# A two-layer hybrid transformer step on one core: rotations and square sums from GpSimd to VectorE, a norm of other instructions, and a second layer with three heads ahead of its norm

## The chip, the core and the metric

One core of a Trainium2 chip runs the whole step in one launch. The engines named below are TensorE (PE, with its weight loads PEld), VectorE (DVE), ScalarE (ACT), GpSimd (POOL) and SyncE (SP), which issues the DMAs. Times are microseconds on the device; lower is better. The metric is the device time of one execution, median of several runs.

## The reference, cut to what matters

Two layers run over 384 tokens of width 1024: 128 context tokens and 256 latent tokens, which share all weights but have their own modulation vectors (shift, scale, gate). Of one layer, for the latent tokens (for the context tokens the same, without rotation and cache):

```python
sa, ca, ga, sm, cm, gm = jnp.split(mod_s, 6, axis=-1)
h = _rmsnorm(xs, norm_mix[d]) * (1.0 + ca) + sa
q, k, v, gb, gc, xin, u, vs = _project(h, w_in[d])
q = _apply_axial_rope(q, rope)
k = _apply_axial_rope(k, rope)
k_all = jnp.concatenate([cache_k[:, d].astype(k.dtype), k], axis=1)
v_all = jnp.concatenate([cache_v[:, d].astype(v.dtype), v], axis=1)
att = _diff_attention(q, k_all, v_all, lam, subln[d], lam_init)
conv = gb * _short_conv(gc * xin, conv_w[d], conv_b[d])
cmlp = _chunk_mlp(u, vs, w_s[d], b_s[d])
xs = xs + ga * (jnp.concatenate([att, conv, cmlp], axis=-1) @ w_out[d])
h = _rmsnorm(xs, norm_mlp[d]) * (1.0 + cm) + sm
xs = xs + gm * _mlp(h, w_up[d], w_down[d])
```

There are four heads with two 64-wide components each. Attention takes, for each component, a softmax over the keys, and combines the two as p0 - lambda * p1. The MLP is a squared ReLU of width 4096.

## The kernel before, in words

**Layout.** Activations are kept transposed: `x` is 128 partitions x 8 tiles (`kt` or `dt`) x 384 tokens. Products have nearly fp32 accuracy: each operand is split into a high and a low part (`hh`, `hl` for activations, `whi`, `wlo` for weights), and `mm3` (L216 to L222) issues three matmuls, high by high, high by low, low by high. Weights come as chunks of 512 KB (`raw`, six buffers); ACT casts a chunk to `whi` (L201), and two ticks later DVE subtracts to get `wlo` (L203), four buffers each. A chunk's successor is begun where the chunk has been used (`refill`).

**What sets the order.** All engines but SP run their instructions in the order in which the program writes them down. That order comes from a heap of Python generators: `start(gen, delay)` puts one in, `go` runs one up to its next `yield`, and `tick()` advances the clock by one after each three-matmul step of a projection (in `proj_tokens` with a width of 512: four ticks for a tile `kt`, nine matmuls). A `yield n` gives the generator its next turn n ticks later. The table `WAIT` holds all these delays as (first layer, second layer). So a delay decides where an instruction stands in its engine's queue, and in that queue it blocks everything behind it until its inputs are there.

**A layer.** The K and Q projections of the first `NPRE` heads ("pkq") do not wait for the norm: they multiply x * scale as it is, with the shift as two more columns (386 instead of 384), and 1/rms (`rstd`) is applied when the result leaves PSUM (`evict`, L514 to L522; `evict_all` L628). Their heads are then finished by `first_heads` (L695 to L713): bias on ACT (L705, L710, L711), `keys` (L660), `queries` (L679). Meanwhile `normed` (L355 to L378) overwrites `hh` and `hl`, tile by tile, with the normed activations: on DVE two products x * scale * rstd, one for each token group (L361), on ACT two halves that add the shift and round to `hh` (L369), on DVE two subtractions to `hl` (L372). From there all projections read the normed parts: V for all heads ("nat", L433 to L455), the remaining heads (`later_heads`, "pk" and "pq", L715 to L726), the convolution, the chunk mixer, then the output projection (three products "po" or "po2"), the up projection ("pup") and the down projection ("pdn").

**Heads.** `keys` rotates K's latent part (`rope_apply`, L652 to L658: a shuffle on DVE, two products and a sum on GpSimd), casts it on ACT (kh, L673, L676) and subtracts on DVE (kl, L677); `queries` does the same for Q (qs, L689, L692). `attention(h, u)` (L730) treats the 128 tokens of unit u: scores (L737, or L740 and L741), maxima on DVE (nm, L745), exponentials on ACT with their sums (e, L750), the two components combined on ACT and DVE (L756, L758), transposes on PE (pt, L762), copies on ACT (atp, ats, L771, L773), and after unit 2 the product with V (po, L785). Units start every 8 ticks and heads every 24, from `unit0` ticks after the start of V on. Score tiles, transposes and statistics share three PSUM buffers ("misc"); projections share four ("acc").

**Square sums.** `stat_tile` (L327 to L336) squares a tile of x on ACT (sq, L329) and adds it to `sacc`; in the MLP parts the add is done by GpSimd (L336), and a product with ones (pstat, L346), two activations (L349, L350) and three DVE instructions (L340 to L342) turn it into `rstd`.

**Hidden units.** `hidden` (L917 to L930) copies two shift columns (`ub`, on DVE), multiplies by `rstd` (DVE), applies ReLU with that bias and a square on ACT, and splits into `ah` and `al`.

Of the kernel before, what the change touches and what calls it, by code (L numbers as in the profile page):

```python
# [15 lines left out]
P = 128  # L16
# [12 lines left out]
NPRE = (3, 2)  # L29
# [33 lines left out]
    "fh0": (14, 14),  # L63
# [8 lines left out]
    "normed": (3, 3),  # L72
    "wait_normed": (1, 12),
    "mix": (4, 4),
    "heads": (4, 1),
# [4 lines left out]
    "unit0": (24, 24),  # L80
    "head": (24, 24),
    "late": (0, 5),
# [18 lines left out]
def dit_kernel(ctx, tc, xT, cT, wmod, wmodT, wall, ck, cv, ws, lam, bs_in, small, rope, ident_in, yT, kT_out, v_out):  # L101
# [112 lines left out]
    def temp(name):  # L214
        return work.tile([P, T], F32, name=name, tag="tA", bufs=4)
# [111 lines left out]
    def stat_tile(dt, eng=nc.gpsimd):  # L327
        sq = temp("sq")
        nc.scalar.activation(sq, x[:, dt, :], AF.Square)  # L329
# [14 lines left out]
    def rstd_of_x():  # L344
        pm = misc_tile("pstat")
        mm(pm[:, 0:T], ones_d, stat["acc"], start=True, stop=True)  # L346
        y = stat["rstd"] = work.tile([P, T], F32, name="rstd", bufs=1)
# [7 lines left out]
    def normed(scale, shift, every):  # L355


        def times(dt):
            t = temp("t")
            for g, a, b in GROUPS:  # L360
                nc.vector.scalar_tensor_tensor(  # L361
                    t[:, a:b], x[:, dt, a:b], scale[:, dt, g : g + 1], stat["rstd"][:, a:b], ALU.mult, ALU.mult
                )
            return t

        t = times(0)
        for dt in range(KT):
            for g, a, b in GROUPS:
                nc.scalar.activation(hh[:, dt, a:b], t[:, a:b], AF.Identity, bias=shift[:, dt, g : g + 1])  # L369
            ahead = times(dt + 1) if dt + 1 < KT else None  # L370
            for g, a, b in GROUPS:
                nc.vector.scalar_tensor_tensor(  # L372
                    hl[:, dt, a:b], t[:, a:b], shift[:, dt, g : g + 1], hh[:, dt, a:b].bitcast(F32),
                    ALU.add, ALU.subtract,
                )
# [132 lines left out]
    for d in range(DEPTH):  # L508
# [26 lines left out]

        if d == 0:
# [42 lines left out]
            for f in range(PARTS - 1):  # L581
# [12 lines left out]
                for dt in (2 * f, 2 * f + 1):  # L594
                    stat_tile(dt, eng=nc.vector)
                if f == 0:
                    next(spread)
            for dt in (KT - 2, KT - 1):
                stat_tile(dt, eng=nc.vector)
# [7 lines left out]
            start(shifted(), 1)  # L607
            start(steps(spread, 4, 3), wt["spread"])
            start(rstd_of_x(), wt["rstd"])
            q_t, k_t, v_t, cv_t, wsT, vsn = mixer_tiles()  # L610
# [12 lines left out]
        else:  # L623
# [4 lines left out]
            def evict_all(i):  # L628
                nc.vector.tensor_copy(bias[:, i], pre[i][:, T:TE])
                evict(i)  # L630

            for i in range(2):
                start(once(evict_all, i), 1 + i)

# [9 lines left out]
        def split_y(i, yf):  # L644
            nc.scalar.copy(y[:, 0, i], yf)
            yield wt["sy"]
            nc.vector.tensor_sub(y[:, 1, i], yf, y[:, 0, i].bitcast(F32))

        LO, HI = slice(0, 64), slice(64, 128)
        parts = {}  # L650

        def rope_apply(t):  # L652
            rt = work.tile([P, 2, TS], F32, name="rt", tag="rope", bufs=1)
            s, t1 = rt[:, 0], rt[:, 1]
            nc.vector.stream_shuffle(s, t, [(i + 16) % 32 for i in range(32)])
            nc.gpsimd.tensor_mul(t1, t, rp[:, 0])
            nc.gpsimd.tensor_mul(s, s, rp[:, 1])
            nc.gpsimd.tensor_add(t, t1, s)  # L658

        def keys(h):  # L660


            k = k_t[:, h % 3]
            nc.sync.dma_start(k[:, TP : 2 * TP], ck[d, h])
            nc.sync.dma_start(kT_out[d, h], k[:, 0:TP])
            yield wt["k0"]
            rope_apply(k[:, 2 * TP :])
            yield wt["k1"]
            kh = work.tile([P, 2, T], F32R, name="kh")
            kl = kl_t[h % 2]  # L670
            parts[h] = [kh, kl]
            for c, own in enumerate((LO, HI)):
                nc.scalar.copy(kh[own, c], k[own, TP:])  # L673
            yield wt["k2"]
            for c, (own, other) in enumerate(((LO, HI), (HI, LO))):
                nc.scalar.copy(kh[other, c], k[own, TP:])  # L676
                nc.vector.tensor_sub(kl[own, c], k[own, TP:], kh[own, c].bitcast(F32))  # L677

        def queries(h):  # L679


            q = q_t[:, h % 3]
            yield wt["q0"]
            rope_apply(q[:, TP:T])
            yield wt["q1"]
            qs = work.tile([P, 2, TS], F32R, name="qs")
            parts[h].append(qs)
            for c, own in enumerate((LO, HI)):
                nc.scalar.copy(qs[own, c], q[own, TP:T])  # L689
            yield wt["q2"]  # L690
            for c, (own, other) in enumerate(((LO, HI), (HI, LO))):
                nc.vector.tensor_sub(qs[other, c], q[own, TP:T], qs[own, c].bitcast(F32))  # L692

        def first_heads():
            for h in range(NPRE[d]):  # L695
                if h != 1:
                    if d == 0:
                        yield from shift_products(raws, bias, 2 * h, 2 * h + 4 - h)
                    qb = bias[:, 2 * h + 1 : 2 * h + 4 - h : 2]
                    nc.vector.tensor_scalar_mul(qb, qb, 0.125)  # L700
                if h == 2:
# [409 lines left out]
```

## Time and profile before

| | |
|---|---|
| time, median of 3 runs | 910.35 (909.78 to 910.5) |
| the profiled execution | 911.23 |
| its span in the profile | 909.4 |
| granted TensorE clock, mean of the span | 0.994 |
| instructions | 14510 |
| share busy: PE, DVE, ACT, POOL | 97%, 72%, 53%, 9% |
| share of the chain that ended last: PE, DVE, ACT, POOL | 84%, 7%, 3%, 2% |
| weights and data read | 153 MB, 171 GB/s over the span |

All places are given in microseconds from the start of the span. The first layer's input side lies at about 56 to 130, the second layer's begins at about 473 and lasts to about 600. A row of a timeline reads: start, duration, engine, line, operation, output<-input, shape, how many alike stand in it, and in square brackets the idle time of the engine ahead of it with what ended that. Where a row holds several instructions ("x2"), its duration is for all of them. A matmul's duration is longer than its place in the pipeline: the distance from one start to the next is what it costs.

### The profile page before, as it was taken

To read this page: it belongs to the slowest core of one execution; us is meant where nothing else is said; L and a number is where in the kernel's file an instruction comes from. 1 tells how busy PE (TensorE), PEld (TensorE's weight loads), DVE (VectorE), ACT (ScalarE), POOL (GpSimd) and SP (SyncE) were. 2 spreads that over 40 slices of the span, in tenths; PEclk is the share of its full clock that TensorE was granted. 3 is DMA by queue.
4 is the path that set the end of the run, shared out by engine and by line. 5 is a ranking of instruction groups with operands and counts; after the bars stand their busy time and mean duration, and the time that the engine had idled before them with its cause. 6 is when DMAs were issued, how large, how long until landed. Compare 5 with 4: busy or idle time off the path is not lost.

```text
span 909.4 us, 14510 instructions
## 1 busy us (share of the span) xinstructions
PE 881.9 (97%) x5476; PEld 841.0 (92%) x5476; DVE 651.5 (72%) x1214; ACT 480.9 (53%) x949; POOL 84.2 (9%) x84
## 2 busy tenths in 40 slices
PE   5999999999999999999999899999999999999996
PEld 4766888999999999999998789999999999999995
DVE  4688887789888878889979878558886334555333
ACT  4458765356762226663336786544776223665331
POOL 1004420011000000000112340002000000000021
PEclk9999999999999999999999999999999999999998
DMA  9877657545657665566673323224565343433302
GB/s 341 298 275 265 194 199 258 179 158 170 217 188 226 220 221 183 174 202 224 223 236 100 120 86 115 74 98 134 185 215 177 116 138 118 127 129 117 115 1 70
DMA packets 48470, 156.55 MB, mean 172 GB/s; under 512 B 5392, under 2 KB 11024, under 8 KB 48400
## 3 DMA queue, kind: packets, MB, share of 16 engines
q1 hardware_dynamic: 48400, 155.63, 51.5%
q8 instruction: 43, 0.70, 0.3%
q14 instruction: 27, 0.22, 0.1%
HBM read 152.98 MB, written 2.62 MB: 171 GB/s over the span
## 4 chain that ended last, share of the span: by engine, by line
PE 84%; DVE 7%; ACT 3%; POOL 2%; issue 2%; DMA 1%; SPq 0%; DVEq 0%; ACTq 0%; POOLq 0%
PE pdn L222 10%; PE pdn L220 10%; PE pdn L221 10%; PE pup L221 10%; PE pup L220 9%; PE pup L222 9%; PE po L222 2%; PE po L220 2%; PE po L221 2%; PE pkq L220 2%; PE pm L262 2%; PE pkq L221 2%; PE pkq L222 1%; DVE wlo L203 1%; PE po L785 1%
## 5 line engine op out<-in xcount | busy, mean ns | idle before, releaser
L201 ACT CAST whi<-raw 128x1024 fp32r<-128x1024 f32 x182 | 190.0, 1050 | 287.9 <-PE pdn L221 154.0
L203 DVE TENSOR_TENSOR wlo<-raw,whi 128x1024 fp32r<-128x1024 f32 x182 | 224.4, 1238 | 62.7 <-ACT whi L201 62.6
L220 PE MATMUL pdn<-ah,whi 128*128 128x384 f32 (+2 forms) x528 | 174.7, 331 | 0.0
L221 PE MATMUL pdn<-al,whi 128*128 128x384 f32 (+2 forms) x528 | 174.6, 331 | 0.0
L222 PE MATMUL pdn<-ah,wlo 128*128 128x384 f32 (+2 forms) x528 | 174.6, 331 | 0.0
L220 PE MATMUL pup<-hh,whi 128*128 128x386 f32 x512 | 174.2, 340 | 0.0
L221 PE MATMUL pup<-hl,whi 128*128 128x386 f32 x512 | 173.7, 339 | 0.3
L222 PE MATMUL pup<-hh,wlo 128*128 128x386 f32 x512 | 172.8, 338 | 0.0
L314 DVE SCALAR_TENSOR_TENSOR junk<-raw,cb 128x1024 bf16<-128x1024 f32 x112 | 136.5, 1219 | 0.4
L221 PEld LDWEIGHTS pdn<-al,whi 128*128 128x128 f32 x528 | 99.2, 188 | 0.0
L220 PEld LDWEIGHTS pdn<-ah,whi 128*128 128x128 f32 x528 | 99.2, 188 | 0.0
L222 PEld LDWEIGHTS pdn<-ah,wlo 128*128 128x128 f32 x528 | 99.2, 188 | 0.0
L221 PEld LDWEIGHTS pup<-hl,whi 128*128 128x128 f32 x512 | 96.9, 189 | 1.1 <-DVE hl L387 0.9
L220 PEld LDWEIGHTS pup<-hh,whi 128*128 128x128 f32 x512 | 96.4, 188 | 0.3
L222 PEld LDWEIGHTS pup<-hh,wlo 128*128 128x128 f32 x512 | 96.5, 188 | 0.0
L336 POOL TENSOR_TENSOR sacc<-sacc,sq 128x384 f32<-128x384 f32 x23 | 29.1, 1266 | 668.8 <-ACT sq L329 534.0
L926 ACT ACTIVATE relu<-relu,ub 128x128 f32<-128x128 f32 (+1 forms) x128 | 51.1, 446 | 17.4 <-DVE relu L923 17.4
L398 DVE SCALAR_TENSOR_TENSOR x<-pdn,modv,x 128x128 f32<-128x128 f32 (+1 forms) x62 | 23.0, 412 | 43.9 <-PE pdn L222 43.9
L930 DVE TENSOR_TENSOR al<-relu,ah 128x384 fp32r<-128x384 f32 x64 | 35.5, 554 | 15.0 <-ACT ah L928 14.8
L220 PE MATMUL po<-y,whi 128*128 128x384 f32 x128 | 43.0, 336 | 0.0
L222 PE MATMUL po<-y,wlo 128*128 128x384 f32 x128 | 42.8, 334 | 0.0
L221 PE MATMUL po<-y,whi 128*128 128x384 f32 x128 | 42.8, 334 | 0.0
(202 smaller groups left out, 1416.3 us busy)
## 6 DMA issues: line engine op xcount, KB each, us to landing
raw<-in_wall_dram SPq DMA_DIRECT2D x182, 512.0 KB, 3.6
raw<-in_wmodT_dram SPq DMA_DIRECT2D x56, 512.0 KB, 4.2
raw<-in_wmod_dram SPq DMA_DIRECT2D x40, 512.0 KB, 5.4
raws<-in_wall_dram SPq DMA_DIRECT2D x6, 512.0 KB, 7.5
x<-in_xT_dram SPq DMA_DIRECT2D x8, 192.0 KB, 7.3
out_dram<-x SPq DMA_DIRECT2D x4, 256.0 KB, 2.6
mix<-in_cv_dram SPq DMA_DIRECT2D x2, 256.0 KB, 5.3
mix<-in_ws_dram SPq DMA_DIRECT2D x2, 256.0 KB, 5.6
```

The costliest lines, as they stand in the source:

```text
L201: nc.scalar.copy(hi, r)
L203: nc.vector.tensor_sub(lo, r, hi.bitcast(F32))
L220: mm(out, wh[wsl], ah[asl], start=first, stop=False)
L221: mm(out, wh[wsl], al[asl], start=False, stop=False)
L222: mm(out, wl[wsl], ah[asl], start=False, stop=last)
L262: mm(pm[32 * j : 32 * j + 32, own], sct[:, kt, :], w[:, (4 * k + j) * width : (4 * k + j + 1) * width], start=(kt == 0), stop=(kt == KT - 1),)
L314: nc.vector.scalar_tensor_tensor(junk, w, 1.0, cb[:, g], ALU.mult, ALU.mult, accum_out=mr[:, dt, g : g + 1])
L336: eng.tensor_add(stat["acc"], stat["acc"], sq)
L398: nc.vector.scalar_tensor_tensor(x[:, dt, a:b], pacc[:, a:b], gate[:, dt, g : g + 1], x[:, dt, a:b], ALU.mult, ALU.add)
L785: mm(po[:, i * P : i * P + P], at, vv, start=(j == 0), stop=(j == len(pairs) - 1))
L926: nc.scalar.activation(r[:, s0:s1], r[:, s0:s1], AF.Relu, bias=ub[:, g : g + 1])
L930: nc.vector.tensor_sub(al[:, i], r, ah[:, i].bitcast(F32))
```

## The change

1. `rope_apply`: the two products and the sum go from GpSimd to DVE and work in place.
2. `stat_tile`: the add to `sacc` goes from GpSimd to DVE.
3. `normed`: per tile DVE does one product x * rstd of 384 columns and one subtraction (two instructions instead of four); ACT applies scale and shift in place in two halves and then casts to `hh` (three instead of two).
4. `hidden`: the copy of the shift columns goes; `rstd` has two more columns that hold 1.0 (a memset on GpSimd), and the product takes 386 columns.
5. `NPRE` is 3 in the second layer too: heads 0 to 2 have K and Q projected ahead of V, from raw x. Head 0 is finished as soon as its pair of results is out (`first_head(0)`, 4 ticks after the pair), head 1 after its own pair, head 2 from 24 ticks after the third.
6. Delays of the second layer: `wait_normed` 12 to 26, `normed` 3 to 2, `unit0` 24 to 12, `late` 5 to 0. The order of convolution and later heads becomes that of the first layer, with the weight chunks packed in that order.

The diff, cut to its core (the functions of the heads are only moved up, and `first_head` is the body of the old loop):

```diff
-NPRE = (3, 2)
+NPRE = (3, 3)
...
-    "wait_normed": (1, 12),
+    "wait_normed": (1, 26),
...
-    "unit0": (24, 24),
+    "unit0": (24, 12),
...
-            eng.tensor_add(stat["acc"], stat["acc"], sq)
+            nc.vector.tensor_add(stat["acc"], stat["acc"], sq)
...
+        stat["rstd1"] = work.tile([P, TE], F32, name="rstd", bufs=1)
+        nc.gpsimd.memset(stat["rstd1"][:, T:TE], 1.0)
+        y = stat["rstd"] = stat["rstd1"][:, 0:T]
...
-            for g, a, b in GROUPS:
-                nc.vector.scalar_tensor_tensor(
-                    t[:, a:b], x[:, dt, a:b], scale[:, dt, g : g + 1], stat["rstd"][:, a:b], ALU.mult, ALU.mult
-                )
+            nc.vector.tensor_mul(t, x[:, dt], stat["rstd"])
...
-                nc.scalar.activation(hh[:, dt, a:b], t[:, a:b], AF.Identity, bias=shift[:, dt, g : g + 1])
+                nc.scalar.activation(
+                    t[:, a:b], t[:, a:b], AF.Identity, bias=shift[:, dt, g : g + 1], scale=scale[:, dt, g : g + 1]
+                )
+            nc.scalar.copy(hh[:, dt, 0:T], t)
             ahead = times(dt + 1) if dt + 1 < KT else None
...
+            nc.vector.tensor_sub(hl[:, dt, 0:T], t, hh[:, dt, 0:T].bitcast(F32))
...
-            nc.gpsimd.tensor_mul(t1, t, rp[:, 0])
-            nc.gpsimd.tensor_mul(s, s, rp[:, 1])
-            nc.gpsimd.tensor_add(t, t1, s)
+            nc.vector.tensor_mul(t, t, rp[:, 0])
+            nc.vector.tensor_mul(s, s, rp[:, 1])
+            nc.vector.tensor_add(t, t, s)
...
             for i in range(2):
                 start(once(evict_all, i), 1 + i)
+            start(first_head(0), wt["heads"])
...
-            for i in (2, 3):
+            for i in range(2, 2 * NPRE[d]):
                 pre.append(proj_tiles(a, 1, TE, "pkq", later=wt["later"]))
                 evict_all(i)
+                if i == 3:
+                    start(first_head(1), 1)
+            start(first_head(2), wt["fh0"])
...
-                ub = work.tile([P, 2], F32, name="ub")
-                nc.vector.tensor_copy(ub, pt[:, T:TE])
-                nc.vector.tensor_mul(r, pt[:, 0:T], stat["rstd"])
+                nc.vector.tensor_mul(r, pt[:, 0:TE], stat["rstd1"])
...
-            chunks += kq[n:] + convs[0] + convs[1]
+        chunks += convs[0] + kq[n:] + convs[1]
```

What that makes of the instruction order is shown at three places of the second layer. First DVE's queue where the norm begins. A row has line, operation, output<-inputs and size; the numbers behind names only tell one tile from another. Before (`mix` is where K and Q of the first heads are put, `t` the first product of the norm):

```order
L629 COPY bias1_4927<-pkq_4930 128x2
L521 SCALAR_TENSOR_TENSOR mix_4928<-pkq_4930,rstd_4968 128x384
L629 COPY bias1_4927<-pkq_5006 128x2
L519 TENSOR_TENSOR mix_4928<-pkq_5006,rstd_4968 128x128
L519 TENSOR_TENSOR mix_4928<-pkq_5006,rstd_4968 128x256
L361 SCALAR_TENSOR_TENSOR t_5062<-x_74,amix1_94,rstd_4968 128x128
L361 SCALAR_TENSOR_TENSOR t_5062<-x_74,amix1_94,rstd_4968 128x256
L361 SCALAR_TENSOR_TENSOR t_5067<-x_74,amix1_94,rstd_4968 128x128
L361 SCALAR_TENSOR_TENSOR t_5067<-x_74,amix1_94,rstd_4968 128x256
L372 SCALAR_TENSOR_TENSOR hl_98<-t_5062,modv1_92,hh_97 128x128
```

And now, where L545 to L548 are a rotation, L567 and L582 the subtractions for kl and qs, and L363 the norm's product:

```order
L203 TENSOR_TENSOR wlo_5059<-raw_5056,whi_5058 128x1024
L702 COPY bias1_4857<-pkq_5031 128x2
L518 TENSOR_TENSOR mix_4858<-pkq_5031,rstd_4898 128x128
L518 TENSOR_TENSOR mix_4858<-pkq_5031,rstd_4898 128x256
L545 STREAM_SHUFFLE rt_5089<-mix_4858 128x256
L546 TENSOR_TENSOR mix_4858<-mix_4858,rp_77 128x256
L547 TENSOR_TENSOR rt_5089<-rt_5089,rp_77 128x256
L548 TENSOR_TENSOR mix_4858<-mix_4858,rt_5089 128x256
L567 TENSOR_TENSOR kl1_105<-mix_4858,kh_5076 64x384 x2
L363 TENSOR_TENSOR t_5104<-x_74,rstd_4898 128x384
```

The norm began behind the third eviction (`pkq_5006`, K of head 1); now it begins behind the fifth (`pkq_5031`, K of head 2) and behind rotations and the subtractions of heads 0 and 1.

Second, DVE's queue from the end of the norm to the maxima of head 0's first unit. Before, a weight subtraction and the rotation and subtractions of head 1's keys stand between the last normed tile (`hl_98<-t_5211`) and the maxima (`nm_5273`):

```order
L372 SCALAR_TENSOR_TENSOR hl_98<-t_5211,modv1_92,hh_97 128x128
L372 SCALAR_TENSOR_TENSOR hl_98<-t_5211,modv1_92,hh_97 128x256
L203 TENSOR_TENSOR wlo_5219<-raw_5216,whi_5218 128x1024
L655 STREAM_SHUFFLE rt_5246<-mix_4928 128x256
L677 TENSOR_TENSOR kl1_105<-mix_4928,kh_5240 64x384 x2
L745 TENSOR_REDUCE nm_5273<-sc_5261 128x1
L745 TENSOR_REDUCE nm_5273<-sc_5262 128x1
```

Now only a weight subtraction (`wlo_5209`) stands between the last normed tile (`hl_98<-t_5203`) and the same maxima (`nm_5232`):

```order
L363 TENSOR_TENSOR t_5190<-x_74,rstd_4898 128x384
L374 TENSOR_TENSOR hl_98<-t_5176,hh_97 128x384
L203 TENSOR_TENSOR wlo_5182<-raw_5179,whi_5181 128x1024
L363 TENSOR_TENSOR t_5203<-x_74,rstd_4898 128x384
L374 TENSOR_TENSOR hl_98<-t_5190,hh_97 128x384
L374 TENSOR_TENSOR hl_98<-t_5203,hh_97 128x384
L203 TENSOR_TENSOR wlo_5209<-raw_5206,whi_5208 128x1024
L752 TENSOR_REDUCE nm_5232<-sc_5225 128x1
L752 TENSOR_REDUCE nm_5232<-sc_5226 128x1
```

The work on head 1's keys has moved ahead of the norm. The first unit's maxima still stand behind the whole norm, though the unit is begun after 12 ticks and not 24.

Third, PE's queue at the scores of head 0's unit 1, with what each instruction waits for in brackets. Before, the scores came behind the last V product and had K of head 2 (`pk_5321`) behind them:

```order
L448 MATMUL nat_5095<-whi_5124,hh_97 128x512
L449 MATMUL nat_5095<-wlo_5125,hh_97 128x512
L450 MATMUL nat_5095<-whi_5124,hl_98 128x512
L740 MATMUL sc_5305<-kh_5147,qs_5206 128x384
L741 MATMUL sc_5305<-kl0_104,qs_5206 128x384
L740 MATMUL sc_5306<-kh_5147,qs_5206 128x384 [waits Activation_49]
L741 MATMUL sc_5306<-kl0_104,qs_5206 128x384
L220 MATMUL pk_5321<-hh_97,whi_5152 128x384 [waits PE_49]
```

Now the same scores stand after the fifth of V's eight tiles, and V goes on behind them:

```order
L447 MATMUL nat_5155<-whi_5117,hh_97 128x512
L448 MATMUL nat_5155<-wlo_5118,hh_97 128x512
L449 MATMUL nat_5155<-whi_5117,hl_98 128x512
L747 MATMUL sc_5264<-kh_4992,qs_5042 128x384
L748 MATMUL sc_5264<-kl0_104,qs_5042 128x384
L747 MATMUL sc_5265<-kh_4992,qs_5042 128x384 [waits Activation_49]
L748 MATMUL sc_5265<-kl0_104,qs_5042 128x384
L447 MATMUL nat_5153<-whi_5117,hh_97 128x512
```

In both, the second score tile waits for an ACT instruction, the exponentials of unit 0, which read the PSUM buffer that it takes.

More of the change, by code (lines that the diff above doesn't have):

```diff
@@ new lines, in queries @@
+        def queries(h):
+            q = q_t[:, h % 3]
+            yield wt["q0"]
+            rope_apply(q[:, TP:T])
+            yield wt["q1"]
+            qs = work.tile([P, 2, TS], F32R, name="qs")
+            parts[h].append(qs)
+            for c, own in enumerate((LO, HI)):
+                nc.scalar.copy(qs[own, c], q[own, TP:T])
+            yield wt["q2"]
+            for c, (own, other) in enumerate(((LO, HI), (HI, LO))):
+                nc.vector.tensor_sub(qs[other, c], q[own, TP:T], qs[own, c].bitcast(F32))
@@ L660, in keys @@
[L660 to L692, printed above, removed]
```

124 lines of the change are left out of this document (66 added, 58 removed).

## The prediction

> **What bounds the kernel now.** The page comes first: TensorE is busy nearly the whole span, so only its gaps and its clock can be won. The list of what it waited for says how much that is.
>
> ```profile
> PE 881.9 (97%) x5476; PEld 841.0 (92%) x5476; DVE 651.5 (72%) x1214; ACT 480.9 (53%) x949; POOL 84.2 (9%) x84
> ```
>
> ```profile
> PE nat L450 <- DVE hl L372: 2.8, 1, 2.8
> PE po L785 <- ACT ats L773: 2.1, 2, 1.3
> PE sc L740 <- ACT e L750: 1.8, 3, 0.8
> ...
> PE psb L471 <- ACT shb L467: 1.2, 1, 1.2
> PE pkq L221 <- DVE hl L387: 0.5, 1, 0.5
> PE pt L762 <- DVE e L758: 0.4, 1, 0.4
> ```
>
> The columns are total, times, longest. The largest wait that the change touches is one of 2.8 us, in the second layer, where V waits for a normed tile. The table by stretches shows DVE full there and PE's clock (the column ahead of the DMA share) down to 0.83:
>
> ```profile
> 500.00:510.00 10.00, 7.87 (x30) 6.42 (x31) 9.89 (x20) 7.17 (x15) 4.99 (x6) 0.83 0.22 70
> ```
>
> PE's timeline gives what that wait costs:
>
> ```profile
> 502.13 0.79 PE L450 MATMUL nat<-whi,hl 128*128 128x512 f32 x1 [2.80 <-DVE hl L372]
> ...
> 505.26 0.61 PE L737 MATMUL sc<-mix,qp 128*128 128x128 f32 x4
> ...
> 505.94 0.39 PE L449 MATMUL nat<-wlo,hh 128*128 128x512 f32 x1
> 506.17 0.40 PE L450 MATMUL nat<-whi,hl 128*128 128x512 f32 x1
> ```
>
> Seven nat products take 502.13 to 505.26, 0.45 each; at full rate the step is 0.23 (505.94 to 506.17). So the idle 2.80 brings 1.5 more, about 1.7 with the scores behind.
>
> **The second layer, step by step.** The change puts 48 more products (head 2's K and Q on raw x) ahead of V, and the norm behind more DVE work.
>
> ```profile
> 485.95 0.33 PE L220 MATMUL pkq<-hh,whi 128*128 128x386 f32 x1
> ...
> 488.06 0.40 PE L448 MATMUL nat<-whi,hh 128*128 128x512 f32 x1
> ```
>
> Twelve products lie between these rows, 2.11 us, 0.176 each. V started at 488.06; with 48 x 0.176 = 8.4 ahead PE could start it at 496.5. Is a normed tile there? DVE starts the evictions at 479.25 as before:
>
> ```profile
> 479.25 0.16 DVE L629 COPY bias<-pkq 128x2 f32<-128x2 f32 x1 [0.35 <-PE pkq L222]
> 479.32 0.61 DVE L519 TENSOR_TENSOR mix<-pkq,rstd 128x128 f32<-128x128 f32 x2
> ...
> 482.50 0.55 DVE L521 SCALAR_TENSOR_TENSOR mix<-pkq,rstd 128x384 f32<-128x384 f32 x1
> ...
> 490.16 0.44 DVE L655 STREAM_SHUFFLE rt<-mix 128x256 f32<-128x256 f32 x1
> ...
> 494.00 0.73 DVE L372 SCALAR_TENSOR_TENSOR hl<-t,modv,hh 128x128 fp32r<-128x128 f32 x2
> 494.66 1.21 DVE L203 TENSOR_TENSOR wlo<-raw,whi 128x1024 fp32r<-128x1024 f32 x1
> ```
>
> ```profile
> 522.91 1.14 DVE L677 TENSOR_TENSOR kl<-mix,kh 64x384 fp32r<-64x384 f32 x2 [0.16 <-ACT kh L673]
> ```
>
> ```profile
> 529.70 0.42 DVE L692 TENSOR_TENSOR qs<-mix,qs 64x256 fp32r<-64x256 f32 x1 [0.33 <-ACT qs L689]
> ```
>
> Queued instructions overlap by some 0.07, so a K eviction is 0.6, a Q eviction 0.65 with its bias scaling, a wlo 1.14. The rotation on DVE is not in the trace: the shuffle's 0.44 plus three products of 256 columns at 0.42 (the qs row has that length), less overlap, 1.6; bounds 1.3 and, all beside GpSimd, 2.7. Ahead of the first normed tile now stand 3 K evictions 1.8, 2 Q evictions 1.3, 4 wlo 4.6, 4 rotations 6.4, 2 kl pairs 2.3 and a qs pair 0.9: 17.3, with 0.2 of waits 17.5. The tile starts at 496.75, done at 497.3. GpSimd's three instructions cost the path nothing more: it has nothing left there.
>
> Then ACT:
>
> ```profile
> 472.21 0.51 ACT L329 ACTIVATE sq<-x 128x384 f32<-128x384 f32 x1
> ...
> 493.41 1.05 ACT L201 CAST whi<-raw 128x1024 fp32r<-128x1024 f32 x1
> 494.36 0.80 ACT L369 ACTIVATE hh<-t,modv 128x128 fp32r<-128x128 f32 x2
> ...
> 510.48 0.37 ACT L750 ACTIVATE e<-sc,nm 128x128 f32<-128x128 f32 x1 [2.19 <-DVE nm L745]
> ```
>
> The convolution's affine has two vector operands, as the new halves have:
>
> ```profile
> 95.06 0.71 ACT L821 ACTIVATE cz<-z,sm 128x385 f32<-128x385 f32 x1
> ```
>
> It is 0.20 over the square's 0.51, 0.10 an operand, so a pair of halves with two is 0.80 + 0.20 = 1.0 (bounds: 0.80 if the second is free, 1.2). With the cast to hh (0.51) a tile holds ACT about 1.4, where 0.8 stood. The first hh is there at 498.8: PE idles 2.3 where it idled 2.8.
>
> The next wait is new. Unit 0 of head 0 now starts after 12 ticks, unit 1 after 20; but its exponential, and DVE's maxima ahead of it, are still queued behind all eight tiles, and the fourth score tile needs a PSUM buffer that only that exponential frees (three in all). ACT's queue from 498.8: seven more tiles 9.8, three whi 2.9, qs 0.8, some 1.2 of hand-offs with DVE: 513.5. Then the last hl 0.5, the wlo that stands before the maxima 1.14, maxima 0.35 and the exponential 0.37: 515.9. PE gets to that score after 45 nat products of 0.231 (10.4) and 0.8 for scores: 510.0. It idles 5.9. Before, it passed there at 510.99 after a gap of 0.60:
>
> ```profile
> 510.99 0.44 PE L740 MATMUL sc<-kh,qs 128*128 128x384 f32 x1 [0.60 <-ACT e L750]
> ```
>
> So it passes 4.9 later. What remains differs: 27 nat products are left, 27 x 0.231 = 6.2, where 48 of K and Q were, 8.4: -2.2. The idle of 5.9 lowers the clock again: +1.7, as the 2.80 did; bounds 0 and 3.4. In the Trainium skill ("TensorE: Matmul & The Clock Gate", "Part 1: The HAM clock gate") the clock halves only after an idle window of about 3.4 us, free-running, and comes back after a busy one. By that rule a gap of 5.9 holds a whole window about 7 times in 10 (an estimate), and in the rest the sum would be 1.7 lower. Here a gap of 2.80 was enough, so the measurement decides and I keep +1.7 in full.
>
> Further on the waits on head 2's keys and queries go, since its work is done early: of the scores' 1.8 the two after 510.99 (1.2), po's second (0.8), pt's 0.4, together 2.2 to 2.4; I take -2.2. But ACT and DVE carry the backlog past 516: unit 2's product of exponentials comes behind V's evictions and whi, and the transposes for it wait; 0 to 2, I take +1.0. The stage: 4.9 - 2.2 + 1.7 - 2.2 + 1.0 = +3.2.
>
> **The rest.** In the first layer the rotation leaves GpSimd as well. ACT waited there for it, and that held ats and with it po (1.3 of its row):
>
> ```profile
> 123.94 0.83 ACT L689 CAST qs<-mix 64x256 fp32r<-64x256 f32 x2 [3.56 <-POOL mix L658]
> ```
>
> On DVE the three products cost 1.3 right behind the shuffle, and the 3.56 goes with po's gap: -1.3 (bounds -1.5 and 0). The psb wait of 1.2 stays, since DVE is as full there. GpSimd beside DVE lengthens DVE's work:
>
> ```profile
> 491.64 1.78 DVE L372 SCALAR_TENSOR_TENSOR hl<-t,modv,hh 128x128 fp32r<-128x128 f32 x2
> ```
>
> ```profile
> 205.28 2.98 DVE L387 SCALAR_TENSOR_TENSOR hl<-x,amlp,hh 128x128 fp32r<-128x128 f32 x4
> ```
>
> The first pair takes 1.78 beside a rotation, 0.73 alone (494.00). The second, four beside the sum of squares, would be 1.4; but the adds come to DVE, 0.55 each (as the Q eviction, of as many columns). At the two starts of the MLP, where pkq's and pup's short waits are, that is worth -0.3 together (bounds -0.6 and +0.3). Within the MLP `hidden` loses a DVE copy (0.16) and gains nothing on PE, which never waits for it there: 0; the cover is an idle DVE. The memset on GpSimd: 0.
>
> **Sum.** +3.2 - 1.3 - 0.3 = +1.6. The profiled run was 911.23 (span 909.4 and 1.83 around it) and lies 0.9 above the median 910.35. It becomes 912.8; on the median, 912.0.
>
> **Rivals.** 1, faster: the normed tiles come early. Against it stands DVE's full queue; for it, that 479 to 500 in the trace holds DVE work stretched by GpSimd (1.78 for 0.73), and my estimate of an ACT tile is not from a row of its own. If the exponential is there by 510.0, there is no second wait, no half clock behind it, no backlog at pt: -1.0 - 2.2 - 2.2 = -5.4, with the rest -1.6, 903.4; if it comes by 512.8 with the clock whole, 1.8 - 2.2 - 2.2 - 1.6 + 1.0 = -3.2, 907.2. Centre 904.5 to 907. Chance 0.27.
>
> 2, slower: the long gap costs more than the short one. If the clock stays low for twice as long (another 1.7) and the transposes after unit 2 wait 2 and not 1, the sum is +4.3 and the time 914.7, or 915.4 with the tile 0.1 dearer (seven times). It decides at the score after 45 nat products: a gap over 4.5 us there, and a granted clock under 0.8 in 515 to 525. Chance 0.18.
>
> 3, no change: cheap hand-offs. With ACT's pair at 0.90 (8 x 0.1 less) and no hand-offs (1.2 less) the exponential comes at 513.9, the passage 2.9 later, no backlog: 2.9 - 2.2 + 1.7 - 2.2 - 1.6 = -1.4, 909. Much the same comes out if the long gap leaves the clock whole: 912.0 - 1.7 = 910.3. Chance 0.12, since 2.80 was enough to lower it. The Trainium skill's rule on the window, above, would make that case likelier.
>
> My forecast has the other 0.43; its own range is 909.5 to 914, from the bounds of the tile, the clock and pt.
>
> **Numbers.** 0.2%, 1.8 us, is about what a measurement of this kernel can tell from no change: 908.5 to 912.2 is "same". Faster: rival 1 and a little of rival 3, 0.29. Same: most of rival 3 and half of the forecast, 0.33. Slower: the other half and rival 2, 0.38. The range, 905.0 to 915.5, leaves out some of rival 1's lower end and a tail above, under 0.2.
>
> **What would show it.** Right: a PE gap of 2 to 3 us at the first V product, near 496.5; a second of 5 to 7 us at a score, near 510, released by ACT's exponential; DVE over 0.95 busy from 480 to 500; the clock under 0.9 in a stretch between 510 and 525; no wait for ats near 125. Wrong: if the first normed tile is there by 495, or the exponential by 511, or if PE's gap at the score is released by something other than the exponential; also if the first layer, seen at the start of its output projection, is more than 2 us off before the second layer begins.

## The result: 923.66 against 910.33, slower by 1.5%

The changed kernel takes 923.66 us (median; 923.16 to 925.38), the kernel before 910.33: a ratio of 1.015 with a 95% interval of 1.0136 to 1.0163. The prediction, 912.0 with a range of 905.0 to 915.5, was wrong. The profiled execution took 923.45, its span 921.7, 12.3 longer than before.

Where the time went, by the starts of the first product of each part on PE (`psh`, `pup`, `pkq`, `pup` again) in the two profiled runs:

| stretch | before | after | difference |
|---|---|---|---|
| start to the first shift product (`psh`) | 56.5 | 55.5 | -1.0 |
| first layer's input side, to the first `pup` | 144.4 | 150.3 | +5.9 |
| first MLP, to the second layer's `pkq` | 269.6 | 269.2 | -0.4 |
| second layer's input side, to its `pup` | 156.0 | 164.4 | +8.4 |
| second MLP and end | 283.0 | 282.3 | -0.7 |

Of the 12.3, 5.9 come from the first layer, for which a gain had been forecast, and 8.4 from the second. The -1.0 of the first row is not the change's: in the experiments below that start lies anywhere from 55.0 to 57.4, in kernels whose instructions there are those of the changed kernel (e8, e1). In PE's list of waits the scores stand first now, and transposes of a head's output (`pot`) are new:

```profile
PE sc L747 <- ACT e L757: 7.0, 2, 4.7
PE pm L262 <- DVE sct L136: 5.5, 1, 5.5
PE pot L813 <- DVE o L807: 4.3, 2, 3.2
PE pkq L220 <- ACT hh L382: 3.2, 2, 2.3
PE nat L447 <- ACT hh L372: 2.7, 1, 2.7
PE psb L470 <- ACT shb L466: 2.3, 2, 1.6
```

The stretches of the second layer show that DVE is no longer full (7.29 of 10 where it was 9.89; the stage begins 4.5 later here, and 504.5 to 514.5 has 7.21), though more work has been given to it, and PE's clock falls to 0.66:

```profile
500.00:510.00 10.00, 7.33 (x28) 5.81 (x27) 7.29 (x16) 7.51 (x15) 0.00 (x0) 0.83 0.19 63
510.00:520.00 10.00, 6.84 (x33) 5.36 (x31) 6.75 (x13) 7.65 (x15) 0.10 (x1) 1.00 0.23 84
520.00:530.00 10.00, 8.45 (x27) 6.94 (x28) 7.55 (x18) 7.05 (x19) 0.00 (x0) 0.66 0.39 113
```

On PE's timeline the first row is V's first product, the second the score tile behind unit 0's exponential. The third and fourth lie one product apart at half rate (0.43), the last is head 2's output:

```profile
503.92 0.79 PE L447 MATMUL nat<-whi,hh 128*128 128x512 f32 x1 [2.67 <-ACT hh L372]
...
521.55 0.69 PE L747 MATMUL sc<-kh,qs 128*128 128x384 f32 x1 [4.71 <-ACT e L757]
...
524.49 0.63 PE L449 MATMUL nat<-whi,hl 128*128 128x512 f32 x1
524.92 0.63 PE L447 MATMUL nat<-whi,hh 128*128 128x512 f32 x1
...
568.83 0.87 PE L813 MATMUL pot<-ident,o 128*128 128x128 f32 x3 [3.22 <-DVE o L807]
```

The first layer before had this row at its first score tile that needs an exponential:

```profile
79.71 0.44 PE L740 MATMUL sc<-kh,qs 128*128 128x384 f32 x1 [0.40 <-ACT e L750]
```

After, PE waits 2.26 there and 1.55 soon behind it, and then works at half rate up to 90.65 (0.32 from one 384-column product to the next, where 0.18 is full rate):

```profile
81.46 0.44 PE L747 MATMUL sc<-kh,qs 128*128 128x384 f32 x1 [2.26 <-ACT e L757]
...
84.54 1.01 PE L470 MATMUL psb<-sel,shb 128*128 128x2 f32 x4 [1.55 <-ACT shb L466]
...
89.40 0.52 PE L220 MATMUL pgc<-hh,whi 128*128 128x384 f32 x1
89.72 0.52 PE L221 MATMUL pgc<-hl,whi 128*128 128x384 f32 x1
```

Why the exponential is late is seen best from the norm's subtraction to `hl`, shown here for the first layer's norm alone (50 to 75). Before, DVE stood still 0.2 in front of it:

```profile
L372 DVE SCALAR_TENSOR_TENSOR hl<-t,modv,hh x16: 339/474/1029, 52.2 to 70.7; 128x128 fp32r<-128x128 f32 x8, 128x256 fp32r<-128x256 f32 x8
its engine sat idle before it (us, times) until:
  ACT hh L369: 0.2, 1
```

After, 6.7 in six of eight tiles:

```profile
L374 DVE TENSOR_TENSOR hl<-t,hh x8: 551/559/559, 52.1 to 72.0; 128x384 fp32r<-128x384 f32 x8
its engine sat idle before it (us, times) until:
  ACT hh L372: 6.7, 6
```

So the "shorter" norm saves DVE some 3 us of work in eight tiles (by starts, two pairs of 0.66 a tile against two instructions of 0.47) and makes it stand 6.5 more: everything that stands behind a subtraction in DVE's queue waits with it for ACT's third step. From the stage's first product on PE (`psh`) to the start of the norm's last subtraction it was 14.2; now it is 16.4.

### The profile page after: what moved, and what is told of

It reads as the page before. It is cut to its first block, busy times and chain, and to the rows that moved or that the text cites. A ratio compares the mean times of both kernels' runs of the same rounds, so it can differ in the third digit from the quotient of the medians.

```text
span 921.7 us, 14457 instructions
## 1 busy us (share of the span) xinstructions
PE 886.3 (96%) x5476; PEld 846.4 (92%) x5476; DVE 645.6 (70%) x1196; ACT 491.9 (53%) x965; POOL 6.0 (1%) x17
## 4 chain that ended last, share of the span: by engine, by line
PE 82%; DVE 10%; ACT 4%; issue 2%; DMA 1%; SPq 0%; DVEq 0%; ACTq 0%
PE pup L220 10%; PE pup L221 10%; PE pup L222 10%; PE pdn L222 10%; PE pdn L221 10%; PE pdn L220 10%; PE po L221 2%; PE po L220 2%; PE po L222 2%; DVE wlo L203 2%; PE pm L262 2%; PE pkq L220 1%; ACT whi L201 1%; ACT t L369 1%; PE pkq L221 1%
## 5 line engine op out<-in xcount | busy, mean ns | idle before, releaser
L203 DVE TENSOR_TENSOR wlo<-raw,whi 128x1024 fp32r<-128x1024 f32 x182 | 221.5, 1222 | 61.3 <-ACT whi L201 61.0
L926 DVE TENSOR_TENSOR relu<-pup,rstd 128x386 f32<-128x386 f32 x64 | 35.5, 559 | 41.4 <-PE pup L222 41.2
L929 ACT ACTIVATE relu<-relu 128x128 f32<-128x128 f32 (+1 forms) x128 | 51.3, 449 | 13.7 <-DVE relu L926 13.5
```

The costliest lines, as they stand in the source:

```text
L203: nc.vector.tensor_sub(lo, r, hi.bitcast(F32))
L926: nc.vector.tensor_mul(r, pt[:, 0:TE], stat["rstd1"])
L929: nc.scalar.activation(r[:, s0:s1], r[:, s0:s1], AF.Relu, bias=r[:, T + g : T + g + 1])
```

## Experiments

All times are medians beside the kernel before on the same chip; its own median there lay between 910.34 and 910.76. "L1" and "L2" are the two input sides as in the table (before 144.4 and 156.0, after 150.3 and 164.4), each from the profiled run, so from one execution. The runs are called e1 to e15 by the numbers in their names.

**One part undone.** The norm of before, in the changed kernel (the four DVE and two ACT instructions of `normed` put back):

```diff
-            nc.vector.tensor_mul(t, x[:, dt], stat["rstd"])
...
-            nc.scalar.copy(hh[:, dt, 0:T], t)
...
+                nc.scalar.activation(hh[:, dt, a:b], t[:, a:b], AF.Identity, bias=shift[:, dt, g : g + 1])
```

> The changed kernel with the norm of before (four DVE and two ACT instructions a tile). Theory A: a tile holds ACT 0.8 and not 1.5, DVE 1.3 and not 1.0; in the first layer the last tile is there about 1.4 earlier and the score wait falls under 1, the half clock goes: -4. In the second layer the eight tiles take about 15.5 and not 17.4, -2: about 917.5. Theory D: 922 to 923. If the norm on ACT helps DVE more than it costs, the time rises above 924.

915.51, ratio 1.0054 (1.0035 to 1.0073); L1 144.4, L2 159.4. The first layer is as it was before the change, with the rotations on DVE, and the second has lost 5.0 of its 8.4. These are the stages of an execution of 913.42, 2.1 below the run's median. With the norm of before the kernel is 8.3 of the 13.3 faster, more than any other single edit below gives back. The rotation, put back to GpSimd in the changed kernel:

```diff
-            nc.vector.tensor_mul(t, t, rp[:, 0])
-            nc.vector.tensor_mul(s, s, rp[:, 1])
-            nc.vector.tensor_add(t, t, s)
+            nc.gpsimd.tensor_mul(t1, t, rp[:, 0])
+            nc.gpsimd.tensor_mul(s, s, rp[:, 1])
+            nc.gpsimd.tensor_add(t, t1, s)
```

> The changed kernel with the rotation's three instructions back on GpSimd. Theory A: in the first layer the score wait falls from 2.3 to about 1.2 and the half clock behind it (2.6) goes, po's wait of 1.3 comes back: -2.5 to -3. In the second layer DVE has about 5 us less of its own and 2.5 more from GpSimd beside it, so the norm starts and ends 2 to 3 earlier and the score gap ends as much earlier: together about 918. Theory D, that the second layer's order alone does it: 922 to 923.

924.56, ratio 1.0151 (1.0131 to 1.0172); L1 148.8, L2 165.9. Nothing is won: 1.5 in the first layer, where 2.5 to 3 had been expected, is lost again in the second. Theory A was wrong here, the rotation on DVE is not what delays the exponential in the second layer: without it PE passes that score only 0.6 earlier in the stage (45.9 for 46.5 behind the first `pkq`). In the changed kernel DVE stands 5.7 in the second layer's norm waiting for ACT, so it has slack there.

**One part alone**, in the kernel before. The new norm (the first diff above the other way round):

```diff
+            nc.vector.tensor_mul(t, x[:, dt], stat["rstd"])
...
+            nc.scalar.copy(hh[:, dt, 0:T], t)
...
+            nc.vector.tensor_sub(hl[:, dt, 0:T], t, hh[:, dt, 0:T].bitcast(F32))
```

> The kernel before with the changed norm alone (DVE product and subtraction, ACT two halves with two vector operands and a cast). Theory N, the norm's form: it lengthens the norm on ACT from 0.8 to 1.5 a tile and holds DVE at each subtraction, whatever the rest is; first layer +4 (score wait 1.4 longer, half clock 2.6), second layer +2 to 4: 916 to 918.5. Theory I, interaction: the longer norm costs only where the rotations on DVE take its slack: 910 to 912.

916.49, ratio 1.0068 (1.0053 to 1.0083); L1 149.6, L2 157.2. Theory N holds: 5.2 of the first layer's 5.9 without any other edit, by the same rows as above:

```profile
80.94 0.44 PE L736 MATMUL sc<-kh,qs 128*128 128x384 f32 x1 [1.90 <-ACT e L746]
83.60 1.02 PE L467 MATMUL psb<-sel,shb 128*128 128x2 f32 x4 [1.11 <-ACT shb L463]
```

The rotation alone:

```diff
+            nc.vector.tensor_mul(t, t, rp[:, 0])
+            nc.vector.tensor_mul(s, s, rp[:, 1])
+            nc.vector.tensor_add(t, t, s)
```

> The kernel before with the rotation's three instructions moved to DVE alone. Theory N: with the old norm the rotation on DVE costs what GpSimd beside DVE cost; po's wait of 1.3 in the first layer goes, one of 1.2 at the transposes of the output comes: 909 to 911. If the rotations on DVE are part of the cause by themselves: 913 or more.

912.80, ratio 1.0023 (1.0007 to 1.004); L1 144.6, L2 157.5. A little more than expected, nearly all of it in the second layer. In the first, po's wait of 1.30 is gone, as expected, and in its place stands one of 1.05 at an output's transposes (131.88); the stage is no shorter. The two small parts alone, `stat_tile` on DVE and `hidden` without its copy:

```diff
-            eng.tensor_add(stat["acc"], stat["acc"], sq)
+            nc.vector.tensor_add(stat["acc"], stat["acc"], sq)
...
-                nc.vector.tensor_copy(ub, pt[:, T:TE])
```

> The kernel before with two small parts of the change alone: the square sums on DVE, and the hidden units without the copy of the shift columns. Theory from the stages of all runs so far: the stretch from the first layer's up projection to the second layer is 269.2 with these parts and 269.6 without, that behind the second layer's up projection 282.2 to 282.5 against 282.9: -0.4 and -0.6, about 909.4. If these differences belong to other parts: 910.4.

909.69, ratio 0.9989 (0.9977 to 1.0): the two MLP stretches are 269.2 and 282.3, L1 144.3, L2 156.0. They are worth about 1.1 in the profiled runs; in the median 0.8, at the edge of what can be told. The second layer's order, with norm and rotation both put back in the changed kernel (the edits of the first two experiments together):

> The changed kernel with both the old norm and the rotation on GpSimd: what stays is the second layer's order, the square sums on DVE and the shorter hidden units. Theory N: the first layer is as before; in the second the score gap of about 4 behind unit 0, half a clock window and the 3.3 at the output's transposes stay: +3 to +4, about 914. If order and norm only cost together: 910 to 911.

916.69, ratio 1.0067 (1.0051 to 1.0084); L1 144.4, L2 162.9. The order costs 6.9 in the second layer by itself, twice what was expected, mostly by two gaps, 3.65 at the score tile and this one at head 2's output, with PE's clock at half behind each (3.4 and 6.8 long):

```profile
561.04 0.87 PE L818 MATMUL pot<-ident,o 128*128 128x128 f32 x3 [4.16 <-DVE o L812]
```

DVE's queue ahead of that output tells why: the shuffle of head 3's queries, the first step of their rotation, stands before it and waits for ACT, which first casts a weight chunk and evicts Q (in the changed kernel the shuffle waits the same 1.61, at 564.26).

```profile
556.40 0.01 DVE L550 LOAD_MASK_SELECT rt<-mix  x1 [1.61 <-ACT mix L737]
556.40 0.44 DVE L550 STREAM_SHUFFLE rt<-mix 128x256 f32<-128x256 f32 x1
556.74 1.57 DVE L203 TENSOR_TENSOR wlo<-raw,whi 128x1024 fp32r<-128x1024 f32 x1
558.24 1.08 DVE L770 SCALAR_TENSOR_TENSOR e<-e,s 128x384 f32<-128x384 f32 x1
...
560.34 0.56 DVE L812 TENSOR_TENSOR o<-po,r 128x384 f32<-128x384 f32 x1
```

The parts don't add. The order costs the second layer 6.9 with the old norm and the rotation on GpSimd (162.9 against 156.0), 1.9 with the rotation on DVE (e4's 159.4 against e6's 157.5), 8.7 with the new norm (e3's 165.9 against e5's 157.2). The middle one rests on e4's profiled execution; by the medians of the whole time, with the 0.8 of the small parts taken out, the three are 6.7, 3.8 and 9.1. Alone, norm and order cost the whole time about the same (5.7 in e5, 5.9 in e7); the order undone by itself was not run.

**The score gap.** A fourth PSUM buffer in the second layer:

```diff
+        if turn[1] and turn[0] % 4 == 0:
+            return ps.tile([P, 512], F32, tag="mod", name=name, bufs=1)
```

> The changed kernel with a fourth PSUM buffer for scores, transposes and statistics in the second layer (the bank of the modulation products, idle there). Theory A, backlog: what holds PE is that unit 0's exponential and its product come late (behind the norm on DVE and ACT), so the 4.7 us gap at the second score tile only moves to the transpose of unit 0, nine V products (2.1 us) further on, which needs the product of the exponentials at about 524.3; gap there about 5, the clock halved behind it as before; time down by 1.5 to 2, about 922. Theory B, buffers: the three buffers are the cause; the gap of 4.7 and the half clock behind it (3.3) go, about 915.7.

923.42, ratio 1.0145 (1.013 to 1.016); L2 162.9. The gap is gone from the score and stands at the transpose of unit 0, 5.8 long: theory A. Unit 0 after 16 ticks:

```diff
-    "unit0": (24, 12),
+    "unit0": (24, 16),
```

> The changed kernel with the first unit of the second layer begun after 16 ticks of V and not 12, so that 18 more V products stand between unit 0's scores and those of unit 1. Theory A: PE reaches the second score tile at about 520.9, where the exponential is there at 521.4: gap 0.5 and no half clock behind; -4.2 - 3.3, then a small wait of 0.3 at the transpose: about 916.5. Theory C, that the longer norm and the rotations themselves cost the time and PE must wait for them somewhere: the gap comes back at the transposes or the product with V, about 922.

917.42, ratio 1.0079 (1.0064 to 1.0094); L2 158.6, 5.8 less. The score gap falls from 4.71 to 2.54, where 0.5 was expected (PE reached the tile at 519.1, not 520.9), a gap of 1.61 is new at a later score, and the gap of 3.2 at head 2's output falls to 0.34: four ticks also moved that out of the rotation's way, which nobody had expected.

**The output's transposes**, 7 ticks later in the second layer (`"at10": (3, 4)` to `(3, 11)`):

> The changed kernel with the transposes of a head's output 7 ticks later on PE in the second layer (11 instead of 4 after DVE's product). The wait of 3.2 at head 2's transposes near 569 comes from DVE's queue, where the rotation of head 3's queries stands ahead; PE has other products to do meanwhile: -3.2 to -3.6, about 920. If the wait moves to a later instruction instead: 923.

922.07, ratio 1.0129 (1.0114 to 1.0144); L2 162.9. Only 1.5 is won, where about 3.4 was expected: much of the gap moves to the next instructions that need DVE.

```profile
567.12 0.52 PE L769 MATMUL pt<-ident,e 128*128 128x128 f32 x3 [1.57 <-DVE ra L340]
573.50 0.52 PE L769 MATMUL pt<-ident,e 128*128 128x128 f32 x3 [0.75 <-DVE e L765]
```

**What in the norm costs.** The product two tiles ahead of ACT, in the kernel before with the new norm:

```diff
-            ahead = times(dt + 1) if dt + 1 < KT else None
+            after = times(dt + 2) if dt + 2 < KT else None
```

> The kernel before with the changed norm, DVE's product two tiles ahead of ACT instead of one. If the norm's cost (5.2 in the first layer) is the hand-off, with DVE waiting in order for each tile's cast and ACT for the next product: most of it goes, about 912. If it is ACT's longer time for a tile (1.5 for 0.8): 916 again.

914.06, ratio 1.0032 (1.0018 to 1.0045); L1 147.7, L2 155.9. In between: 1.9 of the 5.2 comes back. The norm's last subtraction begins 15.2 behind the stage's start (14.2 before, 16.1 in e5) and PE passes the score 24.6 behind it (23.2 before, 25.5 in e5), so part is hand-off. PE's idle time in the stage is almost that of before again (3.3; 2.9 before, 5.1 in e5); what is left of the loss goes with the clock, which is halved from 80.45 to 87.28. Then scale and shift on DVE with only the cast on ACT:

```diff
-                nc.scalar.activation(
-                    t[:, a:b], t[:, a:b], AF.Identity, bias=shift[:, dt, g : g + 1], scale=scale[:, dt, g : g + 1]
-                )
+                nc.vector.tensor_scalar(
+                    t[:, a:b], t[:, a:b], scale[:, dt, g : g + 1], shift[:, dt, g : g + 1], ALU.mult, ALU.add
+                )
```

> The kernel before with the changed norm, but scale and shift applied on DVE (two halves with two vector operands) and only the cast on ACT. ACT's time for a tile falls to 0.5, DVE's rises from 1.0 to about 1.7. If ACT's time is what makes the exponential late: first layer 144.4 to 145.5 and no half clock behind the score gap, 910.5 to 912.5. If any form with one more step costs, by its hand-offs or by a full DVE: first layer 148 to 150, 914 to 917.

918.63, ratio 1.0089 (1.0074 to 1.0104); L1 148.9, L2 159.2. ACT's time is thus not the cause by itself: DVE now waits only 1.3 for `hh`, but has the work instead, and the score waits 2.23. What counts is when the last tile leaves both engines: the last subtraction begins 16.3 behind the stage's start here. How the 5.2 divides between ACT's time, the hand-offs and the place where the half clock falls stays open.

**The clock.** Twenty-four products that nobody reads, in the score gap of the changed kernel:

```diff
+                    if (d, h, u, c) == (1, 0, 1, 1):
+                        fill = ps.tile([P, 512], F32, tag="mod", name="fill", bufs=1)
+                        for i in range(24):
+                            mm(fill[:, 0:T], hh[:, 0, 0:P], hh[:, 0, 0:T], start=True, stop=True)
```

> The changed kernel with 24 products more on PE, whose results nobody reads, ahead of the second score tile of head 0's unit 1, in the second layer's gap of 4.7 us. PE then works where it stood still; the exponential comes when it did. If the half clock behind (522 to 527.6) is due to the idle time: it goes, and the second layer is shorter by 2.7 to 3.2 though nothing else is earlier: about 920.6. If the clock falls for another reason, or extra products only cost: 923.5 or more.

923.58, ratio 1.014 (1.012 to 1.016); L2 165.2. One half of the expectation came true: the extra products (first row) keep the clock up, and PE is 2.3 ahead at unit 2's scores (526.7 for 529.0). The other did not: PE gives that back at two transposes and stands at 537 where the changed kernel stood.

```profile
516.09 4.34 PE L750 MATMUL fill<-hh 128*128 128x384 f32 x24
521.66 0.45 PE L751 MATMUL sc<-kh,qs 128*128 128x384 f32 x1 [1.23 <-ACT e L761]
...
530.40 0.52 PE L773 MATMUL pt<-ident,e 128*128 128x128 f32 x3 [0.74 <-DVE e L769]
...
536.87 0.52 PE L773 MATMUL pt<-ident,e 128*128 128x128 f32 x3 [1.29 <-ACT qs L579]
```

So in the second layer's 500 to 537 not PE but the chain over DVE and ACT sets the pace, and the half clock is not the cause of the loss there. The gap is what that chain leaves over; products that nobody reads can't show what useful ones in it would win, as with the later units of e2. The half clock behind head 2's output, longer here (6.8 for 3.4), was not tried.

**A better version.** The changed kernel with the norm of before (first experiment) and units after 16 ticks, and then with the output's transposes 7 ticks later as well:

```diff
-    "unit0": (24, 12),
+    "unit0": (24, 16),
...
-    "at10": (3, 4),
+    "at10": (3, 11),
```

> The changed kernel with the norm of before and the second layer's first unit after 16 ticks. If the score gap (3.8, with half the clock for 3.4 behind it, 1.7 lost) is a matter of the order alone, it goes here as it did with the later units before: second layer 159.4 - 5.3 = 154, first layer 144.4 as before: about 908.5. If the gap comes back at a later score or transpose: 912 to 913.

909.01, ratio 0.9983 (0.997 to 0.9996); L1 144.2, L2 155.4, near the 908.5 and 154 that were expected. The gap at head 2's output is 0.33 here already, so the next run's expectation, which counted on 3.3, had little to win.

> The one before (norm of before, units after 16 ticks) with the transposes of a head's output 7 ticks later in the second layer as well: the gap of 3.3 at head 2's transposes shrinks to about 1.7, as it did alone: -1.5, about 907. If the delay costs at the end of the stage: 908.5 or more.

908.72, ratio 0.9975 (0.9965 to 0.9985); L1 144.3, L2 155.0. It beats the kernel before by a quarter of a per cent, and the run without the later transposes by 0.3, which the intervals don't tell apart. Of its 2.3 in the span, 1.1 are the small parts and 1.0 the second layer. In neither run's trace is the clock halved from 50 to 900, where the kernel before has one such stretch of 3.4. With the affine part on DVE in that place:

> The changed kernel with the affine part of the norm on DVE, units after 16 ticks and the output's transposes 7 ticks later in the second layer. If DVE has room for it: 907 to 909, as with the norm of before in the same place. If DVE, which carries the rotations as well, is full ahead of the norm: 911 to 914.

918.51, ratio 1.0089 (1.0074 to 1.0104); L1 150.5, L2 159.0: dearer than both cases. DVE is busy 9.67, 9.33 and 9.35 of each 10 from 490 to 520, so it is full there, and the first layer alone is 6.1 dearer than before.

## Why the prediction was wrong, step by step

- **The first layer (-1.3 forecast, +5.9 measured): the step that failed.** The text put the norm there at nothing: "the psb wait of 1.2 stays, since DVE is as full there". But `normed` runs in both layers, and the new norm alone costs 5.2 there (e5). The extra 0.6 a tile on ACT had been worked out for the second layer, and eight times that, put into the first layer's queue, would have pointed at the score wait. The gain of 1.3 by the rotation was wrong too: po's wait did go, but the wait at the output's transposes came, and the rotation alone has L1 at +0.2 (e6). The first two rows are before and after, the third is e6:

```profile
125.61 0.94 PE L785 MATMUL po<-mix,ats 128*128 128x128 f32 x6 [1.30 <-ACT ats L773]
136.88 0.52 PE L813 MATMUL pot<-ident,o 128*128 128x128 f32 x3 [1.08 <-DVE o L807]
131.88 0.52 PE L805 MATMUL pot<-ident,o 128*128 128x128 f32 x3 [1.05 <-DVE o L799]
```

  With the half clock the first layer is 7.2 of the 10.7 by which the difference of the spans (12.3) and the forecast (1.6) lie apart. The prediction's own sign for it came: the first layer's output projection starts 4.9 later in the span, where more than 2 was to show that it is wrong.
- **The second layer (+3.2 forecast, +8.4 measured): right in part.** PE's idle time in the stage went from 5.4 to 10.7, and its clock was halved for 13.7 in place of 3.4. The next points take its terms one by one.
- **DVE's backlog ahead of the norm: right.** The first tile was put 17.5 behind the first eviction; it started at 501.74, 17.9 behind 483.80. Rotations took 1.6, V's wait was 2.67 for 2.3 forecast.
- **The price of a tile: right.** Halves 0.99 for 1.0, cast 0.51:

```profile
502.33 0.99 ACT L369 ACTIVATE t<-t,modv,amix 128x128 f32<-128x128 f32 x2 [3.80 <-DVE t L363]
503.35 0.51 ACT L372 CAST hh<-t 128x384 fp32r<-128x384 f32 x1
...
521.04 0.37 ACT L757 ACTIVATE e<-sc,nm 128x128 f32<-128x128 f32 x1 [1.96 <-DVE nm L752]
```

- **The second gap: right in place and cause, a little too small.** With the second layer's evictions 4.55 later the exponential was due at 520.4 and ended at 521.4. The gap was 4.71 for 5.9, since PE came later too, after half clock behind V's wait; the passage came 6.1 later instead of 4.9.
- **The clock, +1.7: too small, and the wrong kind of term.** It was halved for 6.8 there (520.73 to 527.56), 6.0 of it behind the score, not for 3.4, as rival 2 had it; but e13 shows that its loss there is not on the path. In the first layer its place counts: in e1 and e13, whose first layer has the same instructions as the changed kernel's, the stretch of half rate is as long (6.8) but begins 26.2 behind the stage's start and not 28.3. PE then comes later to the second wait (psb), which is 0.65 and not 1.55, and the stage takes 149.3 for 150.3. The Trainium skill ("TensorE: Matmul & The Clock Gate", "Part 1: The HAM clock gate") has the clock halve after an idle window of 3.4 us that runs free of the work. That it runs free agrees: in e4 PE is back at 512.90 after 3.65 idle, works at full rate until 514.3, and then at half until 517.65.

```profile
512.90 0.44 PE L751 MATMUL sc<-kh,qs 128*128 128x384 f32 x1 [3.65 <-ACT e L761]
...
514.31 0.63 PE L452 MATMUL nat<-wlo,hh 128*128 128x512 f32 x1
514.74 0.63 PE L453 MATMUL nat<-whi,hl 128*128 128x512 f32 x1
```

  That a whole window must be idle does not: 2.67 were enough in the changed kernel.
- **The later waits, -2.2: nearly right, by a wrong reading.** Of the scores' 1.8 the text took two waits (1.2) to lie behind 510.99. Only this one does; the 0.40 is the first layer's (79.71). The sum was 2.0, and those waits did go:

```profile
527.44 0.45 PE L740 MATMUL sc<-kh,qs 128*128 128x384 f32 x1 [0.80 <-ACT e L750]
```

- **The wait at unit 2's transposes, +1.0: not there;** 3.2 at head 2's output instead, with 3.4 of half clock behind it, in no term and no rival. The prediction followed the new order up to unit 2 of head 0 and took "I take -2.2" for the rest. But a changed order makes new meetings further on, and each queue had to be read to the end of the stage.
- **The rest: -0.3 forecast, -1.1 measured,** by the small parts.
- **Rivals.** Both signs of rival 2 came, the gap over 4.5 (4.71) and the clock under 0.8 from 515 to 525 (0.79), but its 914.7 misses by 9: its price was a clock that is off the path there, and no rival had the first layer or head 2's output.

## What to carry to other kernels

When a helper changes, walk every place that calls it, with the same sum. Moving a step from a busy engine to its partner saves nothing if the first engine must wait in order for the partner's result: count the hand-offs of a tile, not only the instructions. And before a gap or a slow clock on the busiest engine is called a loss, ask whether the chain that feeds it would have let it run on; filling the gap is a cheap way to see it.

## What the runs showed of the hardware

The clock's half rate comes in stretches that do not follow the idle time directly: behind 2.67 idle it began at once (503.92), behind 3.65 only 1.4 later, and behind 2.07 not at all. The row of that case (V's first products in e3, at 0.23 to 0.34 a step):

```profile
503.00 0.50 PE L447 MATMUL nat<-whi,hh 128*128 128x512 f32 x1 [2.07 <-ACT hh L372]
503.34 0.39 PE L448 MATMUL nat<-wlo,hh 128*128 128x512 f32 x1
```

In the first layer of e12 a shorter idle was enough, with the granted clock at half from 80.45 to 87.28:

```profile
80.03 0.45 PE L736 MATMUL sc<-kh,qs 128*128 128x384 f32 x1 [1.80 <-ACT e L746]
```

So the length of one gap does not decide by itself; where the gap lies matters as well. The granted clock of the traces shows how. From 50 to 880 of the span the half-rate stretches are 3.41, 6.83 or 10.24 long in every trace, and within a trace they start whole multiples of 3.413 apart. That grid cuts the span into windows of 3.41. Of the windows at full rate in the 17 traces, all 22 in which PE was idle for 2.0 or more were followed by half rate, and none with 1.75 or less was; between 1.80 and 1.89 six were and four were not. The gap of 3.65 shows it in two places: in e7 it covers a whole window (first row: PE busy 0.00, clock 1.00) and the half rate begins with PE's work (second row); in e4 it falls into two windows with 1.58 and 2.08 idle (third and fourth row), and only the second is followed by half rate (fifth).

```profile
508.98:512.40 3.42, 0.00 (x0) 0.00 (x0) 3.29 (x9) 1.20 (x4) 0.00 (x0) 1.00 0.54 153
512.40:515.81 3.41, 3.19 (x8) 2.71 (x9) 2.31 (x6) 1.75 (x6) 0.00 (x0) 0.50 0.41 154
...
507.41:510.82 3.41, 1.84 (x9) 1.25 (x7) 3.41 (x9) 2.23 (x4) 0.10 (x1) 1.00 0.19 38
510.82:514.24 3.42, 1.34 (x6) 1.21 (x7) 2.18 (x7) 1.85 (x6) 0.00 (x0) 1.00 0.54 187
514.24:517.65 3.41, 3.41 (x10) 2.58 (x10) 2.54 (x6) 1.69 (x7) 0.00 (x0) 0.50 0.57 168
```

The count holds for this kernel's long products; behind 895, where the last products have 128 columns, 1.06 idle was enough in the kernel before. The place of a gap on the grid may also be why one kernel differs from one execution to the next: e4's seven lay between 912.48 and 918.27, with a mean granted clock of 0.994 in the shortest and 0.988 in the longest, and 0.006 of 915 us is 5.5. That fits; it was not tried.
